# Order of reading and writing in a walked operand: two halves in turn instead of column by column

## The chip, the cores and the metric

The kernel runs on one core of a Trainium2 chip. The time is the device time of one execution in microseconds (us), and the median of the runs is compared. The engines are named as in the profile: PE is TensorE (PEld its weight loads), DVE is VectorE, ACT is ScalarE, POOL is GpSimd, SP is SyncE, which issues the DMAs.

## The reference

A decoder trunk of two layers on 256 tokens of width 1024, in float32. Layer 0 mixes tokens with a recurrent block (RG-LRU), layer 1 with native sparse attention; each is followed by an MLP of width 4096 with a squared ReLU. RMSNorm stands ahead of each part and at the end.

```python
for i in range(DEPTH):                       # DEPTH = 2
    h = _rmsnorm(x, norm_mix[i])
    if i % N_MIXERS == 0:                    # recurrent block
        x = x + _rglru_mixer(h, ...)
    else:                                    # attention, 16 heads of 64, 4 key/value groups
        x = x + _nsa_mixer(h, ...)
    h = _rmsnorm(x, norm_ffn[i])
    x = x + _sq_relu_mlp(h, mlp_w_up[i], mlp_w_down[i])
return _rmsnorm(x, norm_final)

def _sq_relu_mlp(h, w_up, w_down):
    u = jax.nn.relu(h @ w_up)
    return (u * u) @ w_down
...
    # _rglru_mixer: proj = h @ w_in; one half is the gelu branch y, the other a causal convolution xb
    # of width 4; two block-diagonal gates give a and u of the recurrence h[t] = a[t] h[t-1] + u[t]
    return (hs.astype(h.dtype) * y) @ w_out
```

## The kernel before

**Layout.** Activations stand with channels on the 128 partitions and the 256 tokens along the columns. A weight matrix comes in pieces of 128x1024 (512 KB) by DMA into `raw` buffers. Each float32 operand of a large product is split into a high part and the rest: ScalarE (or VectorE) casts `raw` to `whi`, VectorE takes the difference into `wlo`, and activations are split likewise (`hh`/`hl` for the normalised input, `xbh`/`xbl` for the recurrent block's product, `oh`/`ol` for the attention output, `uh`/`ul`, side by side in a tile `uhl`, for the MLP's hidden layer). A product is then three matmuls: high by high, high by rest, rest by high. `mm3` issues them one by one with 256 columns each; `mm2` joins the first two in one matmul of 512 columns.

**Walked operands.** The moving operand of these matmuls isn't read from column 0 to 255. It is seen as two halves of 128 columns ("places", index i) and read column 0 of half 0, column 0 of half 1, column 1 of half 0, and so on. The names in the code are three views of a tile:

```python
def pairs(x):                                   # neighbours: a PSUM bank in its own order
    return x.rearrange("p (a i) -> p a i", i=2)
def walk(x):                                    # the two halves by turns
    return x.rearrange("p (i a) -> p a i", i=2)
```

So the token in column i*128 + a of the operand comes out in column 2a + i of the PSUM bank. Whoever takes the result out of the bank puts it back in order by reading `pairs(bank)` and writing `walk(tile)`, in the order of the bank: each next element goes to the other half of the tile. The scale `rs` (1/RMS for each token, named rstd in the profile) is read through `walk` too. In the MLP there is a second such step: `u` and `uhl` are made from `pairs(t)`, so that the bank of the down projection comes out in token order.

**Stages.** The first stage (recurrent block, to about 75 us) computes eight convolution chunks, four pairs of gates, eight gelu branches and the output projection. The branch's step out of the bank is line L740, the convolution's L679; `product` makes y (L746 gelu, L747 times the state) for two chunks at a time and splits it into `xbh` and `xbl`, which the output projection reads. Then comes the MLP (`up_post`: L796 relu and scale from the bank into t, L801 the square u, L802 its high part, L803 the rest; down projection by `mm2`, L333 and L335, or `mm3`, L328 to L330). The attention stage (about 265 to 376 us) projects keys, values and queries (`cproj` L960, `kchunk` L923, `qchunk` L911, all into the rotating tiles `tt`), computes scores, softmax (L1140, L1143, L1168), transposes and `pv` (L1202), and splits the output into `oh` and `ol`, the operand of the output projection. The second MLP and the final norm end the kernel.

**Order of the work.** Both mixers are put in order by a planner (`Plan`): each piece of work is given with an engine or a choice of engines, an estimated duration, keys that it reads and writes, and a due time; a list schedule with a few forward and backward passes fixes the order on each engine when the program is built. In the MLP the order is written by hand: weight splits are issued by `tick`, some work is put off with `later` and `flush`. The helpers `copy` (L341) and `diff` (L338) record most casts and differences in the planned stages, so their lines cover many tiles.

Of the kernel before, what the change touches and what calls it, by code (L numbers as in the profile page):

```python
# [12 lines left out]
F32 = mybir.dt.float32  # L13
# [6 lines left out]
P = 128  # L20
# [199 lines left out]
def trunk_kernel(ctx: ExitStack, tc: tile.TileContext, x_in, vec_in, const_in, w2_in, wts, out):  # L220
# [15 lines left out]
    def rotation(*ids):  # L236
        while True:
            for i in ids:
                yield bank(i)
# [52 lines left out]
    def later(fn):  # L292
        deferred.append(fn)
# [23 lines left out]
    def pairs(x):  # L317
        return x.rearrange("p (a i) -> p a i", i=2)

    def walk(x):  # L320
        return x.rearrange("p (i a) -> p a i", i=2)

    def walks(x):
        return x.rearrange("p k (i a) -> p k a i", i=2)

    def mm3(ps, wh, wl, xh, xl, start, stop):
        ps = pairs(ps)
# [12 lines left out]
    def copy(o, a):  # L340
        return lambda e: (e.copy if e is act else e.tensor_copy)(o, a)  # L341
# [199 lines left out]
    with ExitStack() as ph:  # L541
# [119 lines left out]
        def conv(m, t):  # L661
            b = nextbank()
            if m < NFINE:
                wh, wl, _ = sec.weight("in", 8 + m, t)
                z, zk = sec.bank(("in", 8 + m), b, zcols), ("ps", b)
                for k in range(KC):
                    def run(e, k=k):
                        w = slice(k * P, (k + 1) * P)
                        mm3(z(), wh[:, w], wl[:, w], hhw[:, k], hlw[:, k], k == 0, k == KC - 1)
                        if m == 0 and k == 1:  # L670
                            keep_warm(8)
                    add("pe", 0.323 + 0.9 * (m == 0 and k == 1), run, r=[("hi0", m, k // 2), ("lo0", m, k // 2), ("hi", m), ("lo", m), hkey[k]],
                        w=[zk], t=m * 0.33 + k * NI * PJ / 2 if m < NI else t + k * PJ / 2)
            else:
                z, zk = sec.proj("in", 8 + m, b, t, PJ)
            t += 4 * PJ
            x, xk = xps[m % 3], ("xp", m % 3)
            bk = ("xb", m)
            add("dve", 0.34, lambda e: e.tensor_tensor(walk(x[:, 3:]), pairs(z()), walk(rs), op=OP.mult), r=[zk, "rs"], w=[xk], t=t)  # L679
            add("act", 0.49, lambda e: e.activation(xb[m], x[:, 3:], AF.Identity, bias=col(V_CB, m), scale=cw(3, m)),  # L680
                r=[xk], w=[bk], t=t)
            for i in range(3):
                add("dve", 0.4, lambda e, i=i: e.scalar_tensor_tensor(xb[m], x[:, i:i + S], cw(i, m), xb[m], op0=OP.mult,  # L683
                                                                      op1=OP.add), r=[xk], w=[bk], t=t)
# [52 lines left out]

        def branch(m, t):
            z, zk = sec.proj("in", m, nextbank(), t, PJ)
            add("dve", 0.34, lambda e: e.tensor_tensor(walk(y_t[m]), pairs(z()), walk(rs), op=OP.mult), r=[zk, "rs"], w=[("y", m)], t=t + 2.6)  # L740

        def product(m, t):
            yk, hk, lk = keys("y", m), keys("xbh", m), keys("xbl", m)
            y, h, l_, x = (pair(z, m) for z in (y_b, xbhw, xblw, t_b))
            yw = y.rearrange("p k (a i) -> p k a i", i=2)
            add("act", 0.53, lambda e: e.activation(y, y, AF.Gelu_apprx_tanh), r=["tab"], w=yk, t=t)  # L746
            add("dve", 0.6, lambda e: e.tensor_tensor(y, y, x, op=OP.mult), r=keys("t", m), w=yk, t=t)  # L747
            add(HI2, copy(h, yw), r=yk, w=hk, t=t)
            add("dve", 0.6, diff(l_, yw, h), r=yk + hk, w=lk, t=t)
# [34 lines left out]
    def mlp(layer, epilogue, first, last=None):  # L784
        with ExitStack() as ph:
            up = ph.enter_context(tc.tile_pool(name="up%d" % layer, bufs=1, side="right"))
            tmp = ph.enter_context(tc.tile_pool(name="mtmp%d" % layer, bufs=2))
            if last:
                xh, xl, ir = (tmp.tile([P, n], F32R, name=a, bufs=1) for a, n in (("xh", S), ("xl", S), ("ir", P)))
            uhl = [up.tile([P, 2 * S], F32R, name="uhl", tag="uhl", bufs=NF) for _ in range(NF)]  # L790
            uh, ul = [walk(x[:, :S]) for x in uhl], [walk(x[:, S:]) for x in uhl]
            zrot = rotation(3, 4, 5, 0, 1, 2)

            def up_post(m, z):
                t = tmp.tile([P, S], F32, name="t", tag="t")
                dve.scalar_tensor_tensor(walk(t), pairs(z), 0.0, walk(rs), op0=OP.max, op1=OP.mult)  # L796
                flush()
                if m >= len(first) - 1:
                    tick(n=2 if m < 16 else 1)
                u = tmp.tile([P, S], F32, name="u", tag="u")  # L800
                act.activation(u, t, AF.Square)  # L801
                act.activation(uh[m], pairs(t), AF.Square)  # L802
                later(lambda: dve.tensor_tensor(ul[m], pairs(u), uh[m].bitcast(F32), op=OP.subtract))  # L803

            for m in range(NF):
                if m >= len(first):
                    z = next(zrot)[:, :S]
                    wh, wl = get("up%d" % layer, m)
                    for k in range(KC):
                        w = slice(k * P, (k + 1) * P)  # L810
                        mm3(z, wh[:, w], wl[:, w], hhw[:, k], hlw[:, k], k == 0, k == KC - 1)
                else:
                    z = first[m]()
                up_post(m, z)
            for m in range(8):
                zf = next(zrot)
                z, zb = zf[:, :S], zf[:, S:]
                seeded = last is not None and m == 7
                if last and m == 6:
                    act.copy(ir, ident)  # L820
                    act.copy(xh, xt[:, 7])
                    diff(xl, xt[:, 7], xh)(dve)
                if seeded:
                    pe.matmul(z, ir, xh, start=True, stop=False)
                    pe.matmul(z, ir, xl, start=False, stop=False)
                for j in range(4):
                    wh, wl = get("dn%d" % layer, m * 4 + j)
                    for k in range(8):
                        w, i = slice(k * P, (k + 1) * P), j * 8 + k
                        if seeded:  # L830
                            mm3(z, wh[:, w], wl[:, w], uh[i], ul[i], False, i == NF - 1)
                        else:
                            mm2(zf, wh[:, w], wl[:, w], uhl[i], uh[i], i == 0, i == NF - 1)
                    if j == 3 and seeded:
                        last(z)
                    elif j == 3:
                        residual(z, m)
                        residual(zb, m)
                        epilogue(m)
                    tick()  # L840
# [8 lines left out]
    with ExitStack() as ph:  # L849
# [26 lines left out]
        identf = cst[:, C_ID:C_ID + P]  # L876
        oht, olt = (at.tile([P, 8 * S], F32R, name=n) for n in ("oh", "ol"))
        ohw, olw = (walks(x.rearrange("p (k s) -> p k s", s=S)) for x in (oht, olt))
        oh, ol = ([x[:, i] for i in range(8)] for x in (ohw, olw))
        NPT_ = 16  # L880
        pTt = at.tile([P, NPT_ * 3 * P], F32, name="pT")
# [23 lines left out]
        def qchunk(c, b, t, step):  # L905
# [2 lines left out]
            x, xk, l_, lk = turn()  # L908
            a, b_ = sa[c % NQ], sb[c % NQ]
            ak, bk = ("sa", c % NQ), ("sb", c % NQ)  # L910
            add("dve", 0.4, lambda e: e.scalar_tensor_tensor(walk(x), pairs(z()), cst[:, C_QS + c:C_QS + c + 1], walk(rs),  # L911
                                                             op0=OP.mult, op1=OP.mult), r=[zk, "rs"], w=[xk], t=t)
            add(HI, copy(a, x), r=[xk], w=[ak, ak + (1,)], t=t + 0.5)
            add(HI, copy(b_, x), r=[xk], w=[bk, bk + (1,)], t=t + 0.5)
# [4 lines left out]
        def kchunk(gp, br, b, t, step):  # L919
            z, zk = proj_t(("ks", "kw")[br], gp, b, t, step)  # L920
            t += 4 * step
            x, xk, l_, lk = turn()
            add("dve", 0.34, lambda e, x=x: e.tensor_tensor(walk(x), pairs(z()), walk(rs), op=OP.mult), r=[zk, "rs"], w=[xk], t=t)  # L923
            x, l_ = two_blocks(x), two_blocks(l_)
            for hf in range(2):
                g = gp * 2 + hf
# [29 lines left out]
        def cproj(i, gp, b, t, step):  # L956
            z, zk = proj_t(("ck", "cv")[i], gp, b, t, step)
            t += 4 * step
            x, xk, _, _ = turn()
            add("dve", 0.34, lambda e, x=x: e.tensor_tensor(walk(x), pairs(z()), walk(rs), op=OP.mult), r=[zk, "rs"], w=[xk], t=t)  # L960
            for hf in range(2):
                g = gp * 2 + hf
                dst = zfs[i][:, g * NB:(g + 1) * NB].rearrange("p n l -> p (n l)")
# [229 lines left out]
        def pv(js, t):  # L1193
            bk, n = [("ps", 7)], len(js)
            o = zview(("o", js[0]), 7, lambda x: x[:, :n * S])
            oj = slice(js[0], js[-1] + 1)
            ow = lambda: o().rearrange("p (k a i) -> p k a i", k=n, i=2)

            def run(e):
                for j in js:  # L1200
# [11 lines left out]
            add("pe", 1.54 * n + 0.35, run, r=[("pT", j % 4 * 4 % NPT_ + i) for j in js for i in range(4)] + [("bd", p) for p in ps] +  # L1212
                [("pc", j // 2 % 2) for j in js] + [("v", h, b) for h in range(2) for b in range(2)], w=bk, t=t)
            ok, lk = ([(x, j) for j in js] for x in ("oh", "ol"))
            add([("act", 0.1 + 0.24 * n, 0.0), ("dve", 0.07 + 0.27 * n, 0.2)], lambda e: copy(ohw[:, oj], ow())(e), r=bk, w=ok,
                t=t + 1.9 * n)
            add("dve", 0.07 + 0.27 * n, lambda e: diff(olw[:, oj], ow(), ohw[:, oj])(e), r=bk + ok, w=lk, t=t + 1.9 * n + 0.3)

        def out_t(half, m, b, t, step):
            wh, wl, wk = weight("o%d" % half, m // 2, t)  # L1220
# [217 lines left out]
```

## Time and profile before

| | |
|---|---|
| time, median of 3 runs | 562.9 us (562.57 to 563.83) |
| the profiled execution | 563.95 us, span of its instructions 561.8 us |
| busy: PE, DVE, ACT, POOL | 550.5, 436.3, 358.0, 40.1 us |
| granted TensorE clock | 0.996 |
| DMA | 103.61 MB, mean 184 GB/s |

The span runs from the first to the last instruction. Busy times are sums over the span; a matmul's busy time reaches past the start of the next one, so TensorE's pace is read from start to start. A group's row gives busy us, the mean ns of one instruction, and the idle time of its engine before it with what ended it.

### The profile page before, as it was taken

The page shows a single profiled execution, that of the slowest core. Times are in us where ns is not written, and L with a number is a line of the kernel's source. Part 1 is how long each engine was busy: PE and PEld are TensorE (multiplying, and loading weights), DVE is VectorE, ACT ScalarE, POOL GpSimd, SP SyncE. Part 2 cuts the span into 40 slices and gives each one's busy share as a digit, 9 for nine tenths or more (in the row PEclk, how much of TensorE's full clock was granted, in tenths as well). Part 3 has the DMA queues.
Part 4 walks back from the last instruction along what each step waited for, and adds up shares of the span by engine and source line. Part 5 has one row for each costly group of instructions (what it writes and reads, how often), then busy time and mean ns, then how long its engine had stood idle before and what let it go on. Part 6 is the DMA issues. An engine that isn't in the chain of part 4 may idle for free.

```text
span 561.8 us, 11456 instructions
## 1 busy us (share of the span) xinstructions
PE 550.5 (98%) x4422; PEld 528.5 (94%) x4422; DVE 436.3 (78%) x888; ACT 358.0 (64%) x670; POOL 40.1 (7%) x55
## 2 busy tenths in 40 slices
PE   9999899999999999999999999999999999999995
PEld 9989899999999999999899998989999999999995
DVE  6899999887788476476849999989988887465532
ACT  7699587777666354354646999977776765353321
POOL 1010000000000131131000000000000000142220
PEclk9999999999999999999999999999999999999998
DMA  8927266576566646655675432263586667556402
GB/s 313 409 90 226 83 225 215 174 234 200 191 194 222 223 161 214 225 167 198 219 229 177 143 104 58 76 211 99 200 239 200 191 213 234 182 187 218 158 1 76
DMA packets 33222, 103.61 MB, mean 184 GB/s; under 512 B 3856, under 2 KB 8080, under 8 KB 33168
## 3 DMA queue, kind: packets, MB, share of 16 engines
q1 hardware_dynamic: 32624, 102.42, 55.5%
q8 instruction: 35, 0.57, 0.4%
q10 hardware_dynamic: 544, 0.46, 0.2%
q14 instruction: 19, 0.16, 0.1%
HBM read 99.23 MB, written 1.05 MB: 179 GB/s over the span
## 4 chain that ended last, share of the span: by engine, by line
PE 73%; DVE 18%; DMA 5%; ACT 2%; issue 1%; SPq 0%; POOL 0%; DVEq 0%; ACTq 0%; POOLq 0%
PE bank L333 19%; PE bank L329 13%; PE bank L330 13%; PE bank L328 13%; PE bank L335 9%; DVE wlo L338 4%; DMA raw<-in_dram 3%; DVE pt L1140 2%; DMA gw<-in_dram 2%; DVE pt L1168 2%; DVE xb L683 1%; DMA pt<-tt 1%; DVE tt L911 1%; DVE t L735 1%; PE bank L1036 1%
## 5 line engine op out<-in xcount | busy, mean ns | idle before, releaser
L328 PE MATMUL bank<-hhl,whi 128*128 128x256 f32 x768 | 212.0, 276 | 0.4 <-DVE tt L960 0.4
L330 PE MATMUL bank<-hhl,wlo 128*128 128x256 f32 x768 | 211.5, 275 | 0.0
L329 PE MATMUL bank<-hhl,whi 128*128 128x256 f32 x768 | 211.5, 275 | 0.0
L333 PE MATMUL bank<-uhl,whi 128*128 128x512 f32 x480 | 157.3, 382 | 0.0
L328 PEld LDWEIGHTS bank<-hhl,whi 128*128 128x128 f32 x768 | 147.7, 192 | 0.6 <-DVE tt L960 0.4
L330 PEld LDWEIGHTS bank<-hhl,wlo 128*128 128x128 f32 x768 | 147.7, 192 | 0.0
L329 PEld LDWEIGHTS bank<-hhl,whi 128*128 128x128 f32 x768 | 147.7, 192 | 0.0
L287 DVE TENSOR_TENSOR wlo<-raw,whi 128x1024 fp32r<-128x1024 f32 x115 | 142.8, 1262 | 1.9 <-ACT whi L278 1.9
L335 PE MATMUL bank<-uhl,wlo 128*128 128x256 f32 x480 | 130.8, 273 | 0.0
L278 ACT CAST whi<-raw 128x1024 fp32r<-128x1024 f32 x116 | 120.0, 1056 | 14.1 <-ACT whi L278 11.0
L333 PEld LDWEIGHTS bank<-uhl,whi 128*128 128x128 f32 x480 | 90.7, 189 | 12.6
L335 PEld LDWEIGHTS bank<-uhl,wlo 128*128 128x128 f32 x480 | 92.2, 192 | 0.0
L338 DVE TENSOR_TENSOR wlo<-raw,whi 128x1024 fp32r<-128x1024 f32 (+2 forms) x72 | 77.1, 1091 | 1.9 <-ACT whi L341 1.8
L341 ACT CAST whi<-raw 128x1024 fp32r<-128x1024 f32 (+2 forms) x64 | 61.1, 969 | 15.4 <-DMA raw<-in_dram 7.3
L538 DVE TENSOR_TENSOR xt<-xt,bank 128x256 f32<-128x256 f32 x54 | 22.3, 419 | 62.2 <-PE bank L335 60.2
L796 DVE SCALAR_TENSOR_TENSOR t<-bank,rstd 128x256 f32<-128x256 f32 x64 | 39.5, 622 | 22.7 <-PE bank L330 22.6
L801 ACT ACTIVATE u<-t 128x256 f32<-128x256 f32 x64 | 26.7, 417 | 45.1 <-DVE t L796 44.9
L803 DVE TENSOR_TENSOR uhl<-u,uhl 128x256 fp32r<-128x256 f32 x64 | 40.8, 638 | 2.7 <-ACT uhl L802 2.6
L802 ACT ACTIVATE uhl<-t 128x256 fp32r<-128x256 f32 x64 | 42.5, 664 | 0.0
L514 ACT ACTIVATE hhl<-xt,vec 128x256 fp32r<-128x256 f32 x8 | 4.1, 508 | 41.4 <-DVE xt L538 41.4
L1143 ACT ACTIVATE pt<-pt,mx 128x128 f32<-128x128 f32 (+1 forms) x64 | 28.6, 449 | 2.0 <-DVE mx L1140 2.0
L1295 ACT ACTIVATE xg<-xt,vec 128x256 f32<-128x256 f32 x7 | 3.6, 508 | 37.7 <-DVE xt L538 37.7
(206 smaller groups left out, 764.1 us busy)
## 6 DMA issues: line engine op xcount, KB each, us to landing
raw<-in_dram SPq DMA_DIRECT2D x171, 512.0 KB, 4.3
raw<-in_dram SPq DMA_DIRECT2D x4, 560.0 KB, 4.5
gw<-in_dram SPq DMA_DIRECT2D x4, 512.0 KB, 9.2
raw<-in_dram SPq DMA_DIRECT2D x6, 256.0 KB, 4.9
y<-in_dram SPq DMA_DIRECT2D x2, 512.0 KB, 7.5
pT<-in_dram SPq DMA_DIRECT2D x2, 512.0 KB, 6.9
xt<-in_dram SPq DMA_DIRECT2D x3, 256.0 KB, 4.9
kl<-tl SPq DMA_DIRECT2D x8, 64.0 KB, 3.8
```

What stands on the lines that cost most here:

```text
L278: (act.copy if eng is None else eng.tensor_copy)(hi_t[i % NSPL][:, :n], raw_of(i)[:, :n])
L287: (eng or dve).tensor_tensor(lo[:, :n], raw_of(i)[:, :n], hi[:, :n].bitcast(F32), op=OP.subtract)
L328: pe.matmul(ps, wh, xh, start=start, stop=False)
L329: pe.matmul(ps, wh, xl, start=False, stop=False)
L330: pe.matmul(ps, wl, xh, start=False, stop=stop)
L333: pe.matmul(ps.rearrange("p (h a i) -> p h a i", h=2, i=2), wh, xhl.rearrange("p (h i a) -> p h a i", h=2, i=2), start=start, stop=False)
L335: pe.matmul(pairs(ps[:, S:]), wl, xh, start=False, stop=stop)
L338: return lambda e: e.tensor_tensor(o, a, h.bitcast(F32), op=OP.subtract)
L341: return lambda e: (e.copy if e is act else e.tensor_copy)(o, a)
L796: dve.scalar_tensor_tensor(walk(t), pairs(z), 0.0, walk(rs), op0=OP.max, op1=OP.mult)
L802: act.activation(uh[m], pairs(t), AF.Square)
L803: later(lambda: dve.tensor_tensor(ul[m], pairs(u), uh[m].bitcast(F32), op=OP.subtract))
```

## The change

Every VectorE and ScalarE instruction that took a tile through `walk` (or a bank or tile through `pairs` beside it) now takes both sides in the other order: all 128 columns of the first half, then all 128 of the second. On the side of the halves it uses the view `parts` (the halves one after the other, that is, the tile in its own order), on the side of the neighbours the view `evens` (all even columns, then all odd ones). Each element goes to the same place as before. The matmuls and their operands' views stay, and so do all arguments to the planner.

```diff
+    def evens(x):
+        return x.rearrange("p (a i) -> p i a", i=2)
+
+    def parts(x):
+        return x.rearrange("p (i a) -> p i a", i=2)
...
 # conv (L679), branch (L740), qchunk (L911), kchunk (L923), cproj (L960), all alike:
-            add("dve", 0.34, lambda e: e.tensor_tensor(walk(x[:, 3:]), pairs(z()), walk(rs), op=OP.mult), r=[zk, "rs"], w=[xk], t=t)
+            add("dve", 0.34, lambda e: e.tensor_tensor(parts(x[:, 3:]), evens(z()), parts(rs), op=OP.mult), r=[zk, "rs"], w=[xk], t=t)
...
 # product
-            y, h, l_, x = (pair(z, m) for z in (y_b, xbhw, xblw, t_b))
-            yw = y.rearrange("p k (a i) -> p k a i", i=2)
+            y, h, l_, x = (pair(z, m) for z in (y_b, xbh_b, xbl_b, t_b))
+            yw = y.rearrange("p k (a i) -> p k i a", i=2)
+            h, l_ = (z.rearrange("p k (i a) -> p k i a", i=2) for z in (h, l_))
...
 # up_post
-                dve.scalar_tensor_tensor(walk(t), pairs(z), 0.0, walk(rs), op0=OP.max, op1=OP.mult)
+                dve.scalar_tensor_tensor(parts(t), evens(z), 0.0, parts(rs), op0=OP.max, op1=OP.mult)
...
-                act.activation(uh[m], pairs(t), AF.Square)
-                later(lambda: dve.tensor_tensor(ul[m], pairs(u), uh[m].bitcast(F32), op=OP.subtract))
+                act.activation(uhp[m], evens(t), AF.Square)
+                later(lambda: dve.tensor_tensor(ulp[m], evens(u), uhp[m].bitcast(F32), op=OP.subtract))
...
 # pv
-            ow = lambda: o().rearrange("p (k a i) -> p k a i", k=n, i=2)
+            ow = lambda: o().rearrange("p (k a i) -> p k i a", k=n, i=2)
...
-            add([("act", 0.1 + 0.24 * n, 0.0), ("dve", 0.07 + 0.27 * n, 0.2)], lambda e: copy(ohw[:, oj], ow())(e), r=bk, w=ok,
+            add([("act", 0.1 + 0.24 * n, 0.0), ("dve", 0.07 + 0.27 * n, 0.2)], lambda e: copy(ohp[:, oj], ow())(e), r=bk, w=ok,
                 t=t + 1.9 * n)
-            add("dve", 0.07 + 0.27 * n, lambda e: diff(olw[:, oj], ow(), ohw[:, oj])(e), r=bk + ok, w=lk, t=t + 1.9 * n + 0.3)
+            add("dve", 0.07 + 0.27 * n, lambda e: diff(olp[:, oj], ow(), ohp[:, oj])(e), r=bk + ok, w=lk, t=t + 1.9 * n + 0.3)
```

(`uhp`, `ulp`, `ohp` and `olp` are the views by `parts` of the tiles that `uh`, `ul`, `ohw` and `olw` walk.)

More of the change, by code (lines that the diff above doesn't have):

```diff
@@ L739, in branch @@
             z, zk = sec.proj("in", m, nextbank(), t, PJ)
-            add("dve", 0.34, lambda e: e.tensor_tensor(walk(y_t[m]), pairs(z()), walk(rs), op=OP.mult), r=[zk, "rs"], w=[("y", m)], t=t + 2.6)
+            add("dve", 0.34, lambda e: e.tensor_tensor(parts(y_t[m]), evens(z()), parts(rs), op=OP.mult), r=[zk, "rs"], w=[("y", m)], t=t + 2.6)
         def product(m, t):
             yk, hk, lk = keys("y", m), keys("xbh", m), keys("xbl", m)
-            y, h, l_, x = (pair(z, m) for z in (y_b, xbhw, xblw, t_b))
-            yw = y.rearrange("p k (a i) -> p k a i", i=2)
+            y, h, l_, x = (pair(z, m) for z in (y_b, xbh_b, xbl_b, t_b))
+            yw = y.rearrange("p k (a i) -> p k i a", i=2)
+            h, l_ = (z.rearrange("p k (i a) -> p k i a", i=2) for z in (h, l_))
             add("act", 0.53, lambda e: e.activation(y, y, AF.Gelu_apprx_tanh), r=["tab"], w=yk, t=t)
@@ L791, in mlp @@
             uh, ul = [walk(x[:, :S]) for x in uhl], [walk(x[:, S:]) for x in uhl]
+            uhp, ulp = [parts(x[:, :S]) for x in uhl], [parts(x[:, S:]) for x in uhl]
             zrot = rotation(3, 4, 5, 0, 1, 2)
@@ L878, in trunk_kernel @@
         ohw, olw = (walks(x.rearrange("p (k s) -> p k s", s=S)) for x in (oht, olt))
+        ohp, olp = (x.rearrange("p (k i a) -> p k i a", i=2, a=P) for x in (oht, olt))
         oh, ol = ([x[:, i] for i in range(8)] for x in (ohw, olw))
@@ L910, in qchunk @@
             ak, bk = ("sa", c % NQ), ("sb", c % NQ)
-            add("dve", 0.4, lambda e: e.scalar_tensor_tensor(walk(x), pairs(z()), cst[:, C_QS + c:C_QS + c + 1], walk(rs),
+            add("dve", 0.4, lambda e: e.scalar_tensor_tensor(parts(x), evens(z()), cst[:, C_QS + c:C_QS + c + 1], parts(rs),
                                                              op0=OP.mult, op1=OP.mult), r=[zk, "rs"], w=[xk], t=t)
@@ L922, in kchunk @@
             x, xk, l_, lk = turn()
-            add("dve", 0.34, lambda e, x=x: e.tensor_tensor(walk(x), pairs(z()), walk(rs), op=OP.mult), r=[zk, "rs"], w=[xk], t=t)
+            add("dve", 0.34, lambda e, x=x: e.tensor_tensor(parts(x), evens(z()), parts(rs), op=OP.mult), r=[zk, "rs"], w=[xk], t=t)
             x, l_ = two_blocks(x), two_blocks(l_)
@@ L959, in cproj @@
             x, xk, _, _ = turn()
-            add("dve", 0.34, lambda e, x=x: e.tensor_tensor(walk(x), pairs(z()), walk(rs), op=OP.mult), r=[zk, "rs"], w=[xk], t=t)
+            add("dve", 0.34, lambda e, x=x: e.tensor_tensor(parts(x), evens(z()), parts(rs), op=OP.mult), r=[zk, "rs"], w=[xk], t=t)
             for hf in range(2):
```

## The prediction

> **What bounds the kernel now.** I read the first part of the page, then a table of stretches, then the waits of TensorE, and at each wait the timelines of the engines around it.
>
> ```profile
> span 561.8 us, 11456 instructions
> PE 550.5 (98%) x4422; PEld 528.5 (94%) x4422; DVE 436.3 (78%) x888; ACT 358.0 (64%) x670; POOL 40.1 (7%) x55
> ...
> 0.00:5.50 5.50, 4.22 (x20) 4.22 (x21) 1.54 (x5) 3.51 (x8) 0.80 (x10) 1.00 0.61 196
> ...
> 62.00:72.00 10.00, 8.49 (x72) 7.96 (x70) 10.00 (x14) 4.58 (x6) 0.00 (x0) 1.00 0.49 159
> 100.00:180.00 80.00, 80.00 (x706) 79.64 (x705) 66.96 (x95) 57.76 (x95) 0.00 (x0) 1.00 0.61 199
> 300.00:345.00 45.00, 44.64 (x416) 42.22 (x415) 44.54 (x235) 39.85 (x135) 0.00 (x0) 1.00 0.35 101
> 345.00:376.00 31.00, 30.06 (x287) 27.46 (x286) 29.29 (x122) 26.62 (x73) 0.00 (x0) 1.00 0.35 114
> ...
> 553.00:562.00 9.00, 2.89 (x22) 2.38 (x20) 3.46 (x8) 1.46 (x6) 0.00 (x0) 0.72 0.34 117
> ```
>
> The rows are: stretch, length, then busy us and count of PE, PEld, DVE, ACT and POOL, granted clock, DMA share, GB/s. TensorE is the bound, at full granted clock. Where most of the changed instructions are (the MLP, 100 to 180 us) it has no gap at all: 80.00/706 = 0.113 us per matmul. VectorE and ScalarE have room there (66.96 and 57.76 of 80). So only the short places where TensorE stands still can give anything: in 62 to 72 us, where VectorE is busy 10.00 of 10.00, and in the attention stage, where it is busy 44.54 of 45.
>
> ```profile
> PE bank L329 <- DVE xbl L338: 1.2, 2, 1.0
> PE bank L328 <- ACT xbh L341: 0.5, 1, 0.5
> PE bank L1036 <- DVE tt L960: 0.4, 1, 0.4
> ```
>
> These waits of TensorE end on an instruction that the change rewrites: the split of the recurrent block's product (xbh, xbl), and tt, a projection scaled out of its bank; a fourth, on the split of the attention output (ol), is shown further down. The waits by the profile are shorter than what is lost, because a matmul's busy time of 0.28 outlasts its turn of 0.11; I therefore count from start to start.
>
> **The change, and the price of one instruction.** It adds and removes no instruction, wait or DMA. The planner's arguments (engine, cost, keys, due time) stay, so the order on every engine stays. Matmuls read the same walked operands. Each changed instruction visits the same elements, its two halves one after the other: the half-by-half sides become contiguous runs of 128, and the other side (a PSUM bank, or t, u, y in SBUF) is read every second element.
>
> ```profile
> L802 ACT ACTIVATE uhl<-t 128x256 fp32r<-128x256 f32 x64 | 42.5, 664 | 0.0
> L801 ACT ACTIVATE u<-t 128x256 f32<-128x256 f32 x64 | 26.7, 417 | 45.1 <-DVE t L796 44.9
> L538 DVE TENSOR_TENSOR xt<-xt,bank 128x256 f32<-128x256 f32 x54 | 22.3, 419 | 62.2 <-PE bank L335 60.2 <-PE bank L330 1.4
> L740 DVE TENSOR_TENSOR y<-bank,rstd 128x256 f32<-128x256 f32 x8 | 4.9, 618 | 0.0
> L338 DVE TENSOR_TENSOR xbl<-y,xbh 128x512 fp32r<-128x512 f32 x4 | 4.4, 1099 | 0.1
> L747 DVE TENSOR_TENSOR y<-y,t 128x512 f32<-128x512 f32 x4 | 2.7, 674 | 0.0
> L341 ACT CAST oh<-bank 128x512 fp32r<-128x512 f32 x4 | 4.4, 1093 | 0.2 <-PE bank L1202 0.2
> L338 DVE TENSOR_TENSOR ol<-bank,oh 128x512 fp32r<-128x512 f32 x4 | 4.4, 1093 | 1.1 <-ACT oh L341 1.1
> ```
>
> The number after the busy time is the mean in ns. L801 and L802 are the same square of the same tile, one written in order and one walked: 417 against 664. On VectorE the same pair is L538 and L740, 419 against 618; at 512 columns L747 and L338 (xbl), 674 against 1099. So walking costs ScalarE 0.25 us per 256 columns and VectorE 0.20.
>
> No row has a stride of two on either engine, so the new price is bounded. The contiguous rows are one end (on VectorE 419 for 256 columns and 674 for 512; on ScalarE 417, and twice 0.25 off what 512 take now); the walked rows, no gain, are a natural other end, and nothing excludes a price beyond them. For SBUF reads I take the contiguous end: L802 shows the whole penalty with only one of its two sides walked, so what costs is the jump of half a tile at each element, and the new pattern only skips its neighbour. For PSUM reads I take the contiguous end too, because L538 reads a bank at the price of an SBUF read, but here the jump was never on the bank's side, so this is the weakest step. [...] VectorE makes one of the four xbh; its price I leave as it is.
>
> In the MLP, 64 each of L796 (bank to t), L802 and L803 get shorter by 0.2 to 0.25; that is some 40 us of engine time, and I count it as nothing, because TensorE has no gap there. A loss would be covered as well, while VectorE stays under 80.
>
> **Place 1, the recurrent block's output.**
>
> ```profile
> 65.56 0.28 PE L330 MATMUL bank<-xbh,wlo 128*128 128x256 f32 x1
> 66.31 0.38 PE L328 MATMUL bank<-xbh,whi 128*128 128x256 f32 x1 [0.48 <-ACT xbh L341]
> 67.72 0.38 PE L329 MATMUL bank<-xbl,whi 128*128 128x256 f32 x1 [1.03 <-DVE xbl L338]
> ...
> 71.95 0.28 PE L328 MATMUL bank<-xbh,whi 128*128 128x256 f32 x1
> 72.44 0.38 PE L329 MATMUL bank<-xbl,whi 128*128 128x256 f32 x1 [0.21 <-DVE xbl L338]
> ...
> 52.05 0.61 ACT L721 ACTIVATE a<-r 128x512 f32<-128x512 f32 x1
> 52.70 0.69 DVE L722 SCALAR_TENSOR_TENSOR t<-a,t 128x512 f32<-128x512 f32 x1
> 60.98 0.62 DVE L740 TENSOR_TENSOR y<-bank,rstd 128x256 f32<-128x256 f32 x1
> 62.35 1.11 DVE L338 TENSOR_TENSOR xbl<-y,xbh 128x512 fp32r<-128x512 f32 x1
> 65.03 0.61 DVE L740 TENSOR_TENSOR y<-bank,rstd 128x256 f32<-128x256 f32 x1
> 66.61 1.06 DVE L338 TENSOR_TENSOR xbl<-y,xbh 128x512 fp32r<-128x512 f32 x1
> ```
>
> At a turn of 0.11, 65.56 to 67.72 loses 2.16 - 0.22 = 1.94 us, and 71.95 to 72.44 another 0.38 (with small ones just before it, 0.6). What VectorE gains before 52.70 I don't count: there it starts as ScalarE's L721 ends (52.05 + 0.61), so it would arrive earlier and wait. From there to the xbl that releases 67.72 stand three L740, the first and the last shown (0.60) and two xbl (0.85): 1.45 earlier. ScalarE's xbh before it is faster by 0.5 as well and no longer last. The second stall has two more L740 and an xbl ahead of it, 0.82, more than the 0.5 I take of it. Place 1: 1.9 us; with dear PSUM reads 0.85 + 0.35 = 1.2. Late next is the same xbl, by the 0.5 that remain.
>
> **Places 2 to 4, attention.**
>
> ```profile
> 277.03 0.60 DVE L960 TENSOR_TENSOR tt<-bank,rstd 128x256 f32<-128x256 f32 x1 [1.40 <-DMA pt<-tt]
> 372.53 1.05 ACT L341 CAST whi<-raw 128x1024 fp32r<-128x1024 f32 x1 [2.43 <-DMA raw<-in_dram]
> 373.48 1.06 ACT L341 CAST oh<-bank 128x512 fp32r<-128x512 f32 x1
> 374.57 1.09 DVE L338 TENSOR_TENSOR ol<-bank,oh 128x512 fp32r<-128x512 f32 x1 [1.09 <-ACT oh L341]
> 375.71 0.38 PE L329 MATMUL bank<-ol,whi 128*128 128x256 f32 x1 [0.74 <-DVE ol L338]
> ```
>
> Place 2: the last tt gains 0.2 itself, and the DMA that it waits for starts after earlier tt's, 0.2 to 0.4 sooner. The stall is the 0.4 shown among the waits; I take all of it. Place 3: oh and then ol stand in line before 375.71, after a whi cast that waited for a weight. They save twice 0.25 and 0.42: 0.9, against a wait of 0.74 shown on ol and a gap on oh just before it. The whi cast stays where the DMA puts it. Place 4: in 300 to 376 TensorE is idle 0.36 + 0.94 - 0.74 = 0.56 us otherwise, with VectorE nearly full; ten tt at 0.2 and two ol at 0.42 are saved in that time, 2.8 us, so I take 0.5. With dear PSUM reads, places 2 to 4 give nothing.
>
> Sum: 1.9 + 0.4 + 0.9 + 0.5 = 3.7 us. The profiled execution took 563.95 us (span 561.8 and 2.15 around it), 1.05 above the median of 562.9; the gain is a difference within its span, so I subtract it from the median: 559.2.
>
> **Rivals.** (1) Every second element of a bank costs as much as walking: only xbh, xbl and uhl gain, 1.2 us, 561.7. For it: no bank was ever read so; against it: L538. (2) A stride of two costs as much as the jump, in SBUF too, or the cost was that of anything not contiguous: no change, 562.9. Against it: nothing direct, but a step of 8 bytes is much nearer to L801's pattern than one of 512. (3) Slower: a bank read at every second element is dearer than walking. With a second penalty as large as ScalarE's for walking, a 256-column read takes 0.25 us more than now, 0.87 instead of 0.62. In place 1 five L740 eat the 1.2; place 2 loses three times 0.25, 0.75; place 3 twice 0.5, 1.0; place 4 ten tt and two ol, 3.5 us, of which some 3.0 reach the end since VectorE has hardly any room: 4.7 us, 567.6. About 24 such reads of 256 columns stand in line, so it decides from 1.2/24 = 0.05 us on, a price of 0.67. (4) Every stall between the start and the end goes, with chains shortened further upstream. TensorE is idle 561.8 - 550.5 = 11.3 us; 1.28 of it lie in the first row of the stretches and 6.11 in the last, where nothing changes, so 3.9 remain, and about a dozen stalls hide 0.28 - 0.11 = 0.17 each, 2.0. That is 5.9 us, 557.0, the low end; some of it is not the change's to take, such as the waits on DMAs.
>
> **How the numbers follow.** My forecast with its upper end (4) 60 in 100, own range 557.0 to 560.8; (1) 20; (2) 9; (3) 11. From 557.0 to 562.9 holds the first, the second and half of the third. A difference of 0.2% (1.1 us) is about what a measurement of this kernel can tell from none; (1) lies on that line, so I split it: faster 0.70, same 0.19, slower 0.11.
>
> **What would show it.** L802 and L801 near 417 both; xbl near 674 and oh near 632; L740, L796 and L960 near 419 (near 618 it is (1), above 670 it is (3)). TensorE's 65.56-to-67.72 stretch should be shorter by about 1.4, and 375.71 come within 0.6 of the matmul before it. The MLP's pace of 0.113 should stand to the third digit. I am wrong if the instructions are short and the stalls are still there, behind a DMA or ScalarE, or if TensorE's pace itself moves.

## The result and the profile after

The changed kernel takes 557.73 us (median of 4 runs, 557.63 to 557.86) against 563.16 us before (4 runs, 562.57 to 563.83): ratio 0.9903, interval 0.9886 to 0.9921, that is 5.4 us less (4.4 to 6.4). The forecast was 559.2 in a range of 557.0 to 562.9. The kernel before ran 44 times more beside the experiments; one of these executions took 704.82 us at a granted clock of 0.753, and the median of the other 43 is 562.88 (562.16 to 564.42), from which the gain is 5.2 us. The first part of the page after, and the stretches, with the same columns as before:

```profile
span 555.5 us, 11507 instructions
PE 547.0 (98%) x4422; PEld 527.0 (95%) x4422; DVE 414.5 (75%) x888; ACT 348.7 (63%) x670; POOL 40.0 (7%) x55
...
62.00:72.00 10.00, 9.46 (x83) 9.27 (x83) 10.00 (x15) 6.03 (x8) 0.00 (x0) 1.00 0.65 204
100.00:180.00 80.00, 80.00 (x697) 79.36 (x696) 58.21 (x92) 54.14 (x93) 0.00 (x0) 1.00 0.62 195
300.00:345.00 45.00, 45.00 (x424) 43.01 (x423) 44.11 (x262) 41.38 (x144) 0.00 (x0) 1.00 0.34 102
345.00:376.00 31.00, 30.75 (x300) 28.64 (x299) 29.15 (x101) 26.17 (x71) 0.00 (x0) 1.00 0.40 137
```

VectorE is busy 21.8 us less and ScalarE 9.3, and TensorE, with the same 4422 matmuls in the same order, passes through 62 to 72 us with 83 matmuls instead of 72. That it has 697 in 100 to 180 us instead of 706 is no slower pace: it is some 3 us ahead, so other matmuls, of other widths, fall into the window. From matmul 600 to matmul 2050 both kernels take 188.6 us.

The page counts 51 instructions more. The traces have them as semaphore instructions of TensorE's queue, 128 instead of 77, and e1 below has 46 of them, so the change does add waits there; the groups of the engines keep their counts. The groups that changed (mean ns of one behind the busy time):

```profile
L804 DVE SCALAR_TENSOR_TENSOR t<-bank,rstd 128x256 f32<-128x256 f32 x64 | 26.9, 422 | 37.1 <-PE bank L336 36.9
L809 ACT ACTIVATE u<-t 128x256 f32<-128x256 f32 x64 | 26.6, 416 | 51.1 <-DVE t L804 49.8 <-DVE uhl L811 1.2
L810 ACT ACTIVATE uhl<-t 128x256 fp32r<-128x256 f32 x64 | 31.1, 486 | 0.0
L746 DVE TENSOR_TENSOR y<-bank,rstd 128x256 f32<-128x256 f32 x8 | 3.4, 431 | 0.0
L344 DVE TENSOR_TENSOR xbl<-y,xbh 128x512 fp32r<-128x512 f32 x4 | 3.0, 742 | 0.0
L344 DVE TENSOR_TENSOR ol<-bank,oh 128x512 fp32r<-128x512 f32 x4 | 2.7, 679 | 0.6 <-ACT oh L347 0.6
L347 ACT CAST oh<-bank 128x512 fp32r<-128x512 f32 x4 | 2.3, 582 | 0.3 <-PE bank L1211 0.3
```

Every bank read is at the price of a contiguous one: L746 431 ns (618 before), ol 679 (1093), oh 582 (1093). The steps that read SBUF at every second element keep a little: the MLP's high part 486 beside 416 for the same square in order (664 before), xbl 742 (1099 before), ScalarE's xbh 789 (1132 before).

TensorE at the places where it stood still, in the timeline of the changed kernel (start, duration):

```profile
64.52 0.28 PE L334 MATMUL bank<-xbh,whi 128*128 128x256 f32 x1
65.33 0.38 PE L335 MATMUL bank<-xbl,whi 128*128 128x256 f32 x1 [0.54 <-DVE xbl L344]
...
69.42 0.28 PE L334 MATMUL bank<-xbh,whi 128*128 128x256 f32 x1
69.53 0.34 PE L335 MATMUL bank<-xbl,whi 128*128 128x256 f32 x1
...
325.01 0.82 PE L1192 MATMUL bank<-cst,pt 128*128 128x128 f32 x6
325.58 0.38 PE L1138 MATMUL bank<-kh,sb 128*128 128x288 f32 x1
...
368.94 0.28 PE L334 MATMUL bank<-oh,whi 128*128 128x256 f32 x1
369.46 0.38 PE L335 MATMUL bank<-ol,whi 128*128 128x256 f32 x1 [0.25 <-DVE ol L344]
```

The first stall of the recurrent block is down from 1.94 us to 0.81 - 0.11 = 0.70, the second is gone, and the last wait on ol is 0.25 instead of 0.74.

Because the two traces hold the same matmuls in the same order, they can be laid side by side, matmul by matmul, and the lead of one over the other read off. The reference here is the profile of the run e1 below, which has the changed MLP and whose planned stages are those of the kernel before. The lead is flat for all of the MLP, also in the kernels whose MLP still walks (the lead at matmul 600 and at 2050 differs by 0.01 us at most), and it grows in steps. The table has these steps in us, in order of time; the last column is the measured difference of the medians to the kernel before.

| kernel | start, to 60 us | place 1, to 78 us | place 2, 277 us | place 4, to 367 us | place 3, to 376 us | median |
|---|---|---|---|---|---|---|
| changed | 1.06 | 1.99 | 0.11 | 1.49 | 0.73 | -5.4 |
| e2, recurrent block | 1.13 | 2.15 | -0.01 | 0.00 | -0.02 | -2.9 |
| e3, attention | 0.41 | 0.00 | 0.11 | 1.45 | 0.87 | -2.7 |
| e4, xbh and xbl | 0.67 | 1.37 | 0.01 | 0.04 | 0.04 | -1.7 |
| e6, oh and ol | 0.25 | 0.06 | -1.11 | 0.93 | 0.98 | -1.9 |
| e7, tt | 0.23 | 0.09 | -0.70 | 0.80 | 0.11 | -1.2 |
| e9, bank reads | 0.45 | 0.88 | 0.11 | 1.46 | 0.97 | -3.8 |
| before | -0.09 | 0.01 | -0.70 | 0.03 | -0.11 | |

### The profile page after: what moved, and what is told of

The parts are those of the page before. It is cut to its first block, busy times and chain, and to the rows that moved or that the text cites. A ratio compares the mean times of both kernels' runs of the same rounds, so it can differ in the third digit from the quotient of the medians.

```text
span 555.5 us, 11507 instructions
## 1 busy us (share of the span) xinstructions
PE 547.0 (98%) x4422; PEld 527.0 (95%) x4422; DVE 414.5 (75%) x888; ACT 348.7 (63%) x670; POOL 40.0 (7%) x55
## 4 chain that ended last, share of the span: by engine, by line
PE 85%; DMA 5%; ACT 5%; DVE 4%; SPq 1%; issue 1%; DVEq 0%; ACTq 0%
PE bank L339 19%; PE bank L335 16%; PE bank L336 16%; PE bank L334 16%; PE bank L341 9%; DMA raw<-in_dram 4%; PE bank L1211 2%; PE bank L1192 2%; DMA y<-in_dram 1%; PE bank L1138 1%; PE bank L1139 1%; DVE wlo L344 1%; ACT whi L347 1%; DVE t L741 1%; PE bank L1045 1%; ACT t L718 1%
## 5 line engine op out<-in xcount | busy, mean ns | idle before, releaser
L278 ACT CAST whi<-raw 128x1024 fp32r<-128x1024 f32 x116 | 118.2, 1039 | 14.5 <-ACT whi L278 11.0
L804 DVE SCALAR_TENSOR_TENSOR t<-bank,rstd 128x256 f32<-128x256 f32 x64 | 26.9, 422 | 37.1 <-PE bank L336 36.9
L810 ACT ACTIVATE uhl<-t 128x256 fp32r<-128x256 f32 x64 | 31.1, 486 | 0.0
L811 DVE TENSOR_TENSOR uhl<-u,uhl 128x256 fp32r<-128x256 f32 x64 | 27.9, 436 | 3.3 <-ACT uhl L810 3.3
```

The source lines that it names most:

```text
L278: (act.copy if eng is None else eng.tensor_copy)(hi_t[i % NSPL][:, :n], raw_of(i)[:, :n])
L810: act.activation(uhp[m], evens(t), AF.Square)
L811: later(lambda: dve.tensor_tensor(ulp[m], evens(u), uhp[m].bitcast(F32), op=OP.subtract))
```

## The experiments

**e1: the MLP alone.**

```diff
-                dve.scalar_tensor_tensor(walk(t), pairs(z), 0.0, walk(rs), op0=OP.max, op1=OP.mult)
+                dve.scalar_tensor_tensor(parts(t), evens(z), 0.0, parts(rs), op0=OP.max, op1=OP.mult)
...
-                act.activation(uh[m], pairs(t), AF.Square)
+                act.activation(uhp[m], evens(t), AF.Square)
```

> The change in the MLP alone (up_post, 64 times three instructions); the recurrent block and attention walk as before. Theory 1 (the gain is TensorE's stalls in the planned stages getting shorter): 563.2 us, no change, though some 35 us of VectorE and ScalarE busy time go. Theory 2 (less busy neighbours let TensorE run faster, or the MLP's own chain counts): a large part of the 5.4 us, 561 or less. Theory 3 (the two profiled runs differ by 1.0 us in TensorE's first 8 us, so part of the gain is the start): any kernel near before would scatter by 1 us without the change.

563.0 us, ratio 0.9997 (0.9988 to 1.0006): no change. Its stretch of the MLP:

```profile
100.00:180.00 80.00, 80.00 (x705) 79.63 (x704) 59.42 (x96) 54.58 (x95) 0.00 (x0) 1.00 0.62 198
```

VectorE falls from 66.96 to 59.42 us there, and TensorE does 705 matmuls instead of 706. The largest part of the saved engine time is worth nothing, and lighter neighbours didn't speed TensorE there. Theory 3, that the start differs by itself, is left open by this run: its eleven executions lie between 562.41 and 563.12.

**e2: the recurrent block alone; e3: attention alone.** The remaining steps walk as before.

```diff
 # e2: L679, L740 and product            # e3: L911, L923, L960 and pv
-  walk(y_t[m]), pairs(z()), walk(rs)     -  walk(x), pairs(z()), ..., walk(rs)
+  parts(y_t[m]), evens(z()), parts(rs)   +  parts(x), evens(z()), ..., parts(rs)
```

> The change in the recurrent block alone (L679, L740, xbh, xbl). Matmul by matmul, the changed kernel gains 2.0 us on the kernel before between 65 and 78 us. Theory 1: 2.0 us less, 561.1, and TensorE in 265 to 376 us as before. Theory 2: hardly anything, 563. If gains are lost again downstream (behind a DMA in attention): less than 1 us.

> The change in attention alone (tt by L911, L923, L960, and oh, ol). The changed kernel gains 3.1 us between 270 and 376 us. Theory 1: 560.0, and this and the recurrent block's part add up to the whole. If the parts overlap, the two gains add up to more than 5.4; if each needs the other, to less.

e2: 559.94 us, ratio 0.9947 (0.9935 to 0.9960), 2.9 us less. e3: 560.18 us, 0.9950 (0.9938 to 0.9963), 2.7 less. They add up to 5.6, the whole within its interval. The table shows each gaining only at its own places, and e2's lead is carried unchanged through the second MLP to the end (3.29 at 78 us, 3.26 at the end). Nothing is lost again behind a DMA.

**e4: xbh and xbl alone (the SBUF reads on the path); e9: all bank reads, with xbh, xbl and uhl as before.**

```diff
 # e4
...
-            yw = y.rearrange("p k (a i) -> p k a i", i=2)
+            yw = y.rearrange("p k (a i) -> p k i a", i=2)
+            h, l_ = (z.rearrange("p k (i a) -> p k i a", i=2) for z in (h, l_))
```

> Only the SBUF reads on the path: xbh and xbl in the recurrent block. This is what the prediction's rival 1 would have left. By the prediction 1.2 us; by turns measured from start to start (xbl 0.95 to 0.61 us, two of them ahead of the first stall, and one more ahead of the second) 0.7 and 0.35, 562.1. If ScalarE's xbh were last, not xbl: 0.25 and 562.9.

> The change in all steps that read a bank (projections of both mixers, the MLP's t, oh and ol); xbh, xbl and uhl, which read SBUF, walk as before. Theory 1: the whole less what xbh and xbl gave alone (1.7 us), plus what the two share at the first stall: 2.3 us in attention by the trace and 0.6 to 1.2 in the recurrent block, 559.0 to 559.9. If a bank read at every second element disturbed TensorE's writing to banks, its pace of 0.113 us in the MLP would move and the time with it.

e4: 561.17 us, 0.9967 (0.9955 to 0.9980), 1.7 less; e9: 558.98 us, 0.9929 (0.9915 to 0.9943), 3.8 less. Together 5.5, so here too the parts add up. By the table e4 gains 1.37 at place 1 and e9 0.88, a little more than the 1.99 of both: they share the stalls. More than half the gain comes from the steps that read a bank. They change on both sides, the bank's and SBUF's; e5 shows that it is the SBUF side that was dear.

**e5: the price of each pattern.** Scratch instructions on the same tiles in the MLP, where nobody waits for them:

```diff
...
+                    dve.tensor_tensor(walk(D), pairs(t), pairs(rs), op=OP.mult)    # written side walked
+                    dve.tensor_tensor(pairs(D), walk(t), pairs(rs), op=OP.mult)    # read side walked
+                    dve.tensor_tensor(parts(D), evens(t), parts(rs), op=OP.mult)   # read, every second
...
+                    act.activation(walk(A), pairs(t), AF.Square)
```

> The changed kernel with two scratch instructions more in each of the MLP's up steps (nothing reads their results): on VectorE a product of t (or the bank) with rstd, on ScalarE a square, 128x256 each, in rotation over forms: all sides in order; only the written side walked; only the read side walked; read or written at every second element; at every fourth; jumping between two places 4 elements apart; the bank read walked and at every second or fourth element. Theory A (what costs is a jump to another small block of SBUF at each element): read side walked and written side walked both cost 620 on VectorE and 660 on ScalarE, every second element costs little, every fourth element costs as much as walking, jumps of 4 elements as well. Theory B (the long distance of the jump costs): every fourth and the short jump are as cheap as in order, 420. Theory C (only the written side costs, since ScalarE's step had only that walked): the read side walked is 420. Banks: every second element 420; walked or every fourth either 420 (a bank doesn't mind) or above 600 (it has blocks too, only larger ones).

It ran once, in 557.15 us. VectorE is busy 71.58 of 80 us in its 100 to 180 us (58.21 in the changed kernel) and the lead of TensorE stays flat there, so this work in the MLP costs nothing either. The groups of that run, in the order: VectorE all in order (L810), written walked (L812), read walked (L814), every second read (L816) and written (L818), short jump written (L820) and read (L822), every fourth written (L824) and read (L826), bank read walked (L828) and every fourth (L830); ScalarE in order (L837), written walked (L839), read walked (L841), every second read (L843), every fourth written (L851) and read (L853), bank read walked (L855) and every fourth (L857).

```profile
L810 DVE TENSOR_TENSOR DD<-t,rstd 128x256 f32<-128x256 f32 x6 | 2.6, 425 | 0.1
L812 DVE TENSOR_TENSOR DD<-t,rstd 128x256 f32<-128x256 f32 x6 | 3.8, 628 | 0.0
L814 DVE TENSOR_TENSOR DD<-t,rstd 128x256 f32<-128x256 f32 x6 | 2.5, 422 | 0.0
L816 DVE TENSOR_TENSOR DD<-t,rstd 128x256 f32<-128x256 f32 x6 | 2.7, 444 | 0.0
L818 DVE TENSOR_TENSOR DD<-t,rstd 128x256 f32<-128x256 f32 x6 | 2.7, 448 | 0.0
L820 DVE TENSOR_TENSOR DD<-t,rstd 128x256 f32<-128x256 f32 x6 | 3.9, 650 | 0.0
L822 DVE TENSOR_TENSOR DD<-t,rstd 128x256 f32<-128x256 f32 x6 | 2.5, 420 | 0.0
L824 DVE TENSOR_TENSOR DD<-t,rstd 128x256 f32<-128x256 f32 x6 | 4.6, 765 | 0.0
L826 DVE TENSOR_TENSOR DD<-t,rstd 128x256 f32<-128x256 f32 x4 | 2.9, 729 | 0.0
L828 DVE TENSOR_TENSOR DD<-bank,rstd 128x256 f32<-128x256 f32 x4 | 1.7, 414 | 0.0
L830 DVE TENSOR_TENSOR DD<-bank,rstd 128x256 f32<-128x256 f32 x4 | 1.7, 416 | 0.0
L837 ACT ACTIVATE AA<-t 128x256 f32<-128x256 f32 x6 | 2.4, 401 | 0.0
L839 ACT ACTIVATE AA<-t 128x256 f32<-128x256 f32 x6 | 4.0, 662 | 0.0
L841 ACT ACTIVATE AA<-t 128x256 f32<-128x256 f32 x4 | 1.9, 473 | 0.0
L843 ACT ACTIVATE AA<-t 128x256 f32<-128x256 f32 x4 | 1.9, 476 | 0.0
L851 ACT ACTIVATE AA<-t 128x256 f32<-128x256 f32 x4 | 3.1, 784 | 0.0
L853 ACT ACTIVATE AA<-t 128x256 f32<-128x256 f32 x4 | 3.1, 769 | 0.0
L855 ACT ACTIVATE AA<-bank 128x256 f32<-128x256 f32 x4 | 1.5, 376 | 1.8 <-DVE DD L828 1.8
L857 ACT ACTIVATE AA<-bank 128x256 f32<-128x256 f32 x4 | 1.5, 379 | 0.2
```

Theory C holds for walking on VectorE: only the walked write costs (628), and a walked read is free (422). On ScalarE most of the cost is the write (662, in order 401), and a walked read costs as much as every second element (473 and 476). The distance doesn't matter (650 written with a jump of 4 elements), which rules out B. A holds for writes and for every fourth element (765, 729, 784, 769), and fails for walked reads. A bank is read at one price in each pattern tried (every second element 416 and 378 in the same run). So what the bank-reading steps saved was the walked write into SBUF.

**e6: oh and ol alone; e7: tt alone.**

```diff
 # e6
...
-            ow = lambda: o().rearrange("p (k a i) -> p k a i", k=n, i=2)
+            ow = lambda: o().rearrange("p (k a i) -> p k i a", k=n, i=2)
...
 # e7, L960 as L911 and L923
-  e.tensor_tensor(walk(x), pairs(z()), walk(rs), op=OP.mult)
+  e.tensor_tensor(parts(x), evens(z()), parts(rs), op=OP.mult)
```

> The change in oh and ol alone. By the traces the wait before the last output products gains 0.73 us (place 3), and the first of place 4's stalls (329 us, 0.5) follows an ol on VectorE. Theory 1: 0.73 + 0.35 and a little, 561.6. If place 4 is all owed to tt: 0.73, 562.1. If the last wait is set by the weight's DMA: under 0.3.

> The change in the attention stage's projections (tt) alone, twelve reads of a bank, each 0.12 us shorter from start to start. Theory 1: what oh and ol leave of attention's 2.3 us by the trace, 1.2 us, 561.7. If TensorE's small stalls all hang on oh and ol: no change, 562.9. Place 2 (the stall at 277 us) is gone in all four earlier profiles, also in the two with attention as before, so it should be gone here without being a gain.

e6: 561.08 us, 0.9960 (0.9946 to 0.9974), 1.9 less; e7: 561.75 us, 0.9978 (0.9969 to 0.9986), 1.2 less. Place 3 belongs to oh and ol (0.98 against 0.11); place 4 gains from either (0.93 and 0.80, together more than the 1.45 of both). The third part of e7's expectation failed: the stall at 277 us is there again, and in e6 longer than before, although e6 left that step alone. TensorE in e6, then in e1:

```profile
276.56 0.29 PE L1045 MATMUL bank<-whi,hhl 128*128 128x304 f32 x1
277.70 0.38 PE L1043 MATMUL bank<-whi,hhl 128*128 128x256 f32 x1 [0.85 <-DVE tt L967]
```

```profile
276.88 0.29 PE L1045 MATMUL bank<-whi,hhl 128*128 128x304 f32 x1
277.01 0.27 PE L1043 MATMUL bank<-whi,hhl 128*128 128x256 f32 x1
```

Both have the walked tt. So that stall differs from one execution to the next (the tt that ends it waits for a DMA). The three profiles that have it are of executions slower than the medians of their kernels: 563.95 against 562.88 (before), 561.98 against 561.08 (e6), 562.47 against 561.75 (e7). Its going away in the changed kernel's profile isn't shown to be the change's doing.

**e8: the walked kernel with its true durations in the planner; e10: the changed kernel likewise.** The kernel before tells its planner 0.34 us for a bank read and 0.6 for xbl. From start to start VectorE's bank read took 0.45 in the kernel before (61.90 to 62.35, where xbl starts) and takes 0.33 now (60.38 to 60.71). Before, then now:

```profile
61.90 0.62 DVE L740 TENSOR_TENSOR y<-bank,rstd 128x256 f32<-128x256 f32 x1
```

```profile
60.38 0.42 DVE L746 TENSOR_TENSOR y<-bank,rstd 128x256 f32<-128x256 f32 x1
60.71 0.77 DVE L344 TENSOR_TENSOR xbl<-y,xbh 128x512 fp32r<-128x512 f32 x1
61.36 1.24 DVE L344 TENSOR_TENSOR wlo<-raw,whi 128x1024 fp32r<-128x1024 f32 x1
```

The estimates thus nearly fit the changed kernel (xbl: 61.36 - 60.71 = 0.65), not the one that they stood in; besides xbh, the cast oh is off in it, 0.48 for 0.58.

```diff
 # e8
-        HI2 = [("act", 0.53, 0.0), ("dve", 0.34, APEN)]
+        HI2 = [("act", 0.94, 0.0), ("dve", 0.47, APEN)]
...
-            add("dve", 0.6, diff(l_, yw, h), r=yk + hk, w=lk, t=t)
+            add("dve", 0.95, diff(l_, yw, h), r=yk + hk, w=lk, t=t)
 # e10
+        HI2 = [("act", 0.69, 0.0), ("dve", 0.36, APEN)]
```

> The kernel before, with nothing changed but the planner's estimates: the walked instructions are given the time that they take from start to start (0.45 instead of 0.34 for a bank read, 0.51 instead of 0.40 for q, 0.94 and 0.47 instead of 0.53 and 0.34 for xbh, 0.95 instead of 0.6 for xbl and ol, 0.88 instead of 0.58 for oh). In the changed kernel the old estimates hold to 0.02 us for all but xbh. Theory 1a (the stalls were planned away by an order that the walked instructions could not keep): the planner finds an order that hides part of it, 561 to 562. Theory 1b (VectorE is simply full in these places, so that no order helps): 563, and by chance of another order up to 1 us either way.

> The changed kernel with the planner's estimates for its dearest remaining steps set to the measured time from start to start: xbh 0.69 instead of 0.53 on ScalarE and 0.36 instead of 0.34 on VectorE, oh 0.48 instead of 0.58. Only the order can change. If the 0.7 us stall that is left at 64.5 us is a matter of order, up to 0.7 us less, 557.0; if VectorE is full there, as the run with the estimates of the kernel before suggests, 557.7, within 0.5 either way.

e8: 562.94 us, ratio 0.9998 (0.9989 to 1.0007). Its order differs, its time doesn't, as theory 1b has it; this is one other order, and that none could help isn't shown. The stalls are in other places, most of them on the same engine (waits of TensorE, and VectorE's stretch):

```profile
PE bank L330 <- DVE wlo L338: 1.3, 2, 0.7
...
PE bank L1129 <- DVE mx L1140: 0.8, 2, 0.6
PE bank L329 <- DVE ol L338: 0.7, 1, 0.7
```

```profile
62.00:72.00 10.00, 8.48 (x71) 7.91 (x70) 9.97 (x13) 5.42 (x6) 0.00 (x0) 1.00 0.65 211
```

e10: 558.32 us, 0.9911 (0.9897 to 0.9925), not below the changed kernel's 557.73; its five executions lie between 557.40 and 558.60. The only lower time is that of e5, the single 557.15, and no run shows a kernel that is faster than the changed one.

## Why the prediction was right, and where its terms were off

- *Only TensorE's stalls count, the MLP gives nothing*: shown by e1, by e5, and by the flat lead of the kernels whose MLP walks (before, e2, e3, e4) against e1, whose MLP doesn't. That no wait is added was wrong, see the 51 above; 46 of them stand in e1, which takes as long as before.
- *Bank reads at the contiguous price* (called the weakest step): right, 416 to 431 ns at 256 columns. Rival 1 and rival 3 fall with it; e9 is worth 3.8 us where rival 1 gave it nothing. No run shows the dear PSUM reads that the places were reckoned with besides: in e5 a bank read walked and at every fourth element took VectorE 414 and 416 ns (L828 and L830) against 425 in order from SBUF, and ScalarE 376 and 379 (L855 and L857) against 401.
- *SBUF reads at the contiguous price*: nearly, for another reason than the one given. I wrote that the jump of half a tile costs; e5 shows that it is the walked write. Rival 2 falls: every second element costs 20 ns on VectorE (444 against 425 in e5), 70 on ScalarE (486 against 416 in the changed kernel), at 256 columns. The 632 ns named for oh is what the working gives for xbh (1132 less twice 0.25 us); xbh came to 789, and oh, for which it gives 593, to 582.
- *Place 1, 1.9 us*: 1.99 measured, partly by luck. I took the saving of an instruction from its duration (0.20), while on a full engine the next one starts earlier by 0.12 only (0.45 to 0.33). The first stall gave 1.94 - 0.70 = 1.24 instead of 1.45; the second and two small ones behind it made up for it. Not counting VectorE's lead before 52.70 was right: with VectorE's instructions laid beside those of the kernel before, its lead falls there from 1.64 to 1.29 us, which is ScalarE's lead.
- *Place 2, 0.4 us*: failed. The stall read in the one profile of before is not in e1, and e7, whose tt is changed, has it again, so there was nothing steady to gain; 0.11 at most shows.
- *Place 3, 0.9 us*: 0.73 to 0.98 in the table, as forecast.
- *Place 4, 0.5 us*: too small by 1.0. I bounded it by idle time in the stretches, 0.56, though I had said that a matmul's busy time hides 0.17 of each stall. One of these stalls, in the kernel before:

```profile
329.06 0.82 PE L1183 MATMUL bank<-cst,pt 128*128 128x128 f32 x6
330.16 0.37 PE L1129 MATMUL bank<-kh,sb 128*128 128x288 f32 x1 [0.28 <-DVE cm L1147]
```

  It was 1.10 us from start to start and is 0.57 now (325.01 to 325.58): 0.53 gained where the profile shows a wait of 0.28.
- *The sum, 3.7 us*: places 1 to 4 come to 1.99 + 0.11 + 1.49 + 0.73 = 4.3 by the table, and to 5.1 in the one profile of e5, which holds the whole change; measured 5.4, of 4.4 to 6.4. The profile of the changed kernel is another 1.06 us ahead by 60 us, a lead that lies anywhere from -0.09 to 1.13 in the profiles and doesn't go with the part of the change that a kernel has. In the changed kernel some 0.3 of it arises at 34 us, a step that e6 and e7 show as well, though their recurrent block walks. The other 0.77 arises in TensorE's first 8 us, where no changed instruction runs: matmuls start 0.21 us apart at first and 0.11 later, and the moment of the turn differs. In e1, then in the changed kernel:

```profile
5.28 0.41 PE L334 MATMUL bank<-hhl,whi 128*128 128x256 f32 x1
5.49 0.42 PE L335 MATMUL bank<-hhl,whi 128*128 128x256 f32 x1
```

```profile
5.57 0.28 PE L334 MATMUL bank<-hhl,whi 128*128 128x256 f32 x1
5.68 0.28 PE L335 MATMUL bank<-hhl,whi 128*128 128x256 f32 x1
```

  The traces' records of the granted clock begin, at full clock, at 7.39 us (before), 6.81 (e1), 5.19 (e2) and 4.23 (changed), and the leads over e1 at 8 us are -0.25, 0, 0.77 and 0.77. In e5 and e10, which hold the whole change too, the records begin at 6.70 and 6.39 and the leads are 0.05 and 0.19. So the start looks like a matter of the execution and not of the change. Whether all four executions of the changed kernel had an early one was not settled, and up to 1.1 of the 5.4 us is open in this way. Of the forecast's own terms, place 2 was 0.3 too large and place 4 was 1.0 too small, and the two errors offset each other in part.

## What to carry to other kernels

Read a stall from the start of one matmul to the start of the next, and an instruction's saving on a full engine from start to start too; busy and idle columns hid part of both here (a stall of place 4 gave 0.53 us where a wait of 0.28 was shown, a bank read of VectorE 0.12 where its duration fell by 0.20). When a result has to be put back in order on its way out of a bank, put the irregular side on the bank and write SBUF in order (VectorE in e5: 414 to 416 ns for a bank read in each pattern tried, 628 for a walked write into SBUF against 425 in order). A stall that ends on a DMA should be seen in a second profile before its price goes into a sum.

## What the runs showed of the hardware that I had not expected

In e5 VectorE and ScalarE read a bank at one price walked, at every second and at every fourth element (414 to 416 and 376 to 379 ns at 256 columns; VectorE in order, L538 of the kernel before, 419). In SBUF reads and writes differ there: VectorE reads two places by turns for nothing (422 against 425) but pays 0.20 us to write them by turns (628); ScalarE pays 0.07 and 0.26 (473 and 662 against 401). Every fourth element costs 0.30 to 0.38 us either way on both (765 and 729 on VectorE, 784 and 769 on ScalarE).
